# A hybrid decoder layer: the first projection piece by kinds of parts, key copies by DMA, and VectorE and GpSimd work given to ScalarE

## Chip, cores and metric

The kernel runs on one core of one Trainium2 chip. The metric is the device time of one execution in microseconds (us). Engine names are those of the profile: PE is TensorE, DVE is VectorE, ACT is ScalarE, POOL is GpSimd, SP is the engine that issues most DMAs; PEld is the loading of weights into TensorE.

## What is computed

One layer over 16 meta tokens and 1024 tokens of width 1024, in float32. Cut to what matters:

```python
u = rmsnorm(h, g_pre_mix)
q, k, v, xr, yr = split(u @ w_in)          # 512, 128, 128, 512, 512 columns
attn = sliding_window_attention_with_sinks(q, k, v, sinks)   # 8 heads of 64, 2 key heads, window 128
xr = causal_depthwise_conv(xr, conv_w, conv_b)               # 4 taps
hr = rg_lru(xr, w_a, b_a, w_x, b_x, lam)                     # gates, then a scan over the tokens
mix = concat([attn, gelu(yr) * hr]) @ w_out
h = h + rmsnorm(mix, g_post_mix)
f = square(relu(rmsnorm(h, g_pre_ffn) @ w_ff1)) @ w_ff2      # 4096 wide
h = h + rmsnorm(f, g_post_ffn)
return h without the meta tokens
```

## The kernel before

**Parts.** Every large operand is held as two float32r tiles: `hi`, the rounded value, and `lo`, what the rounding left. A product is three matmuls into one PSUM bank: hi·hi, hi·lo and lo·hi (`mm3`, L120 to L125; the projections are its lines 123, 124 and 125). As a rule ACT writes `hi` (a cast, L95, or a scaled copy, L116) and DVE writes `lo` (a subtraction, L98 or L117) after it.

**Order.** The engines run their own instructions in order. The order on each engine is fixed when the kernel is built, by a scheduler that looks at the whole program; `behind` and `lut` add pure order edges to it. Tiles come from pools of fixed depth by a letter ("a" 16, "b" 17, "c" 8, "d" 4, "e" 2, "raw" 2, "ws" 4), so a load can start only when the tile's earlier user is done.

**Stage 1, the first projections (0 to about 60 us).** The tokens are cut into four pieces of 256 columns (the first has 272, with the meta tokens). For each piece `normed` (L200 to L202) takes a row tile, squares and sums it on ACT, gets the reciprocal root on POOL (L158 adds EPS, L164 raises to the power -0.5), scales it on DVE; `transposed` (L242) turns it on PE, 8 blocks `kc` of 128 features, and ACT and DVE write the parts of `u` (L116, L117). Then four weights meet the piece: keys `wk`, values `wv`, the first query pair `wq`, the first recurrent chunk `wx`. `project` runs, for each `kc`, the three matmuls of that block. The sinks take the result out of PSUM: `put_k` writes each key head's `hi` into its own half of the partitions (ACT, L303), a second copy of it into the other half (DVE, L304), and its `lo` (DVE, L305). Attention needs both halves, since a query tile carries `hi` in one half and `lo` in the other.

**Stage 2, attention and the other projections (about 60 to 275 us).** For each of 4 head pairs and 2 halves, `scores` makes masked scores, exponentials (ACT, L82), and scales each of its 8 blocks of 128x256 by the reciprocal of the sum on DVE (L480). `attend` turns them and multiplies with the values. The other projections of queries, x and y are laid between as filling. `conv` runs per chunk on DVE: a first step that scales and adds the bias (L530), then three taps.

**Stage 3, recurrence gates, output projection, norms (to about 345 us), and stage 4, the two feed-forward products (to the end).** Both feed-forward products are done in seven block products instead of eight. In the second one, `fetch_2` (L1046 to L1060) loads each step's weight tile; where two tiles are summed, the second is loaded on top of the first by a POOL DMA that adds (L1055), or as a tile of its own. `LASTW` names the pools for the last eight steps.

**End.** The rows come out in two halves. Rows 512 to 1023 are finished during the last steps (`finish_early`). Rows 0 to 511, blocks j = 0 to 3, are finished after the last matmuls (`finish_half`, `finish_late`): add the last product (L788), sum of squares, reciprocal root, scale, add to the residual. For j = 0 and 1 the sum of squares is on ACT (L1117), the root on POOL (L160 on DVE, L164 on POOL), and a POOL DMA adds the block to the output (L1162). For j = 2 and 3 the residual is loaded ahead, the sum of squares is on DVE (L1165), the root on POOL (L1173), and the block is written by two plain DMAs (L1177, L1180). The last block's columns are done in two parts of 256.

Of the kernel before, what the change touches and what calls it, by code (L numbers as in the profile page):

```python
# [37 lines left out]
def hybrid_layer(  # L38
# [76 lines left out]
    def split_scaled(hi, lo, src, scale):  # L115
        nc.scalar.activation(hi, src, AF.Copy, scale=scale)  # L116
        nc.vector.scalar_tensor_tensor(  # L117
            lo, src, scale, f32(hi), op0=ALU.mult, op1=ALU.subtract
        )

    def mm3(dst, lhs, rhs, start, stop):
# [3 lines left out]
        nc.tensor.matmul(dst, ll, rh, start=False, stop=stop, skip_group_check=True)  # L125
# [29 lines left out]
    def rstd_of(ssq_parts, n=P):  # L155
# [8 lines left out]
        nc.gpsimd.tensor_tensor(rs[:n], ms[:n], half_pow[:n], op=ALU.pow)  # L164
# [32 lines left out]
    def norm_rows(src, n):  # L197
        xn = slot("d", [P, D])
        ssq = small.tile([P, 1], F32, name="ssq", tag="ssq")
        nc.scalar.activation(xn[:n], src, AF.Square, scale=RMS_SC, accum_out=ssq[:n])  # L200
        rs = rstd_of([ssq[:n]], n)
        nc.vector.tensor_scalar(xn[:n], src, rs, None, op0=ALU.mult)  # L202
        return xn
# [13 lines left out]

    ALL = [(0, 272), (272, 256), (528, 256), (784, 256)]
    REAL2 = [(16, 512), (528, 512)]

# [14 lines left out]
    def transposed(b, xn):  # L235
        t0, n = ALL[b]
        for kc in range(KC):
# [3 lines left out]
            for s, m in xn:  # L241
                nc.tensor.transpose(  # L242
                    pt[:, o : o + m], s[:m, kc * P : (kc + 1) * P], ident[:m, :m]
                )
                o += m
            uh, ul = u[kc]
            split_scaled(
                uh[:, t0 : t0 + n], ul[:, t0 : t0 + n], pt[:, :n],
                g_mix_col[:, kc : kc + 1],
            )  # L250

# [25 lines left out]
    wk = split_w(rk, "b")  # L277
    wv = split_w(rv, "b")
    transposed(0, xn)
    wq = split_w(rq)  # L280
    wx = split_w(rx)
# [7 lines left out]


    khh = [slot("b", [P, T], F32R) for _ in range(2)]
    kl = [slot("b", [P, T], F32R) for _ in range(2)]

    vk = [slot("b", [P, 8, P], F32R) for _ in range(2)]
    HALF = (slice(0, HD), slice(HD, P))
    vt = slot("c", [P, TT])
    for h in range(2):
        nc.gpsimd.memset(f32(kl[h][HALF[1 - h]]), 0.0)

    def put_k(hh, lo, src):  # L300
        for h in range(2):
            r, o = HALF[h], HALF[1 - h]
            nc.scalar.copy(hh[h][r], src[r])  # L303
            nc.vector.tensor_copy(hh[h][o], src[r])  # L304
            nc.vector.tensor_tensor(lo[h][r], src[r], f32(hh[h][r]), op=ALU.subtract)  # L305

    def sink_k(acc, t0, n):
        o = 0
        if t0 == 0:
            m = slice(0, NMETA)  # L310
            put_k(
                [km[:, 0, m], km[:, 1, m]], [km[:, 2, m], km[:, 3, m]], acc[:, m]
            )
            o = NMETA
        c = slice(t0 + o - NMETA, t0 - NMETA + n)
        put_k(
            [khh[0][:, c], khh[1][:, c]], [kl[0][:, c], kl[1][:, c]], acc[:, o:]
        )

    def sink_v(acc, t0, n):  # L320
        nc.scalar.copy(vt[:, t0 : t0 + n], acc)

    def new_q():
# [3 lines left out]
        def sink_q(acc, t0, n):  # L327
            c = slice(t0 - NMETA, t0 - NMETA + n)
            for h in range(2):
                r, o = HALF[h], HALF[1 - h]  # L330
                split_scaled(q[h][r, c], q[h][o, c], acc[r], HD ** -0.5)
# [10 lines left out]

    q0, sink_q0 = new_q()
    xr0, sink_x0 = new_x("c")
    for b in range(4):
        if b:
            transposed(b, normed(b))
        piece = [ALL[b]]
        project(wk, piece, sink_k)
        project(wv, piece, sink_v)  # L350
        project(wq, piece if b else [(16, 256)], sink_q0)
        project(wx, piece, sink_x0)
# [79 lines left out]
    def scores(j, half, q):  # L432
# [44 lines left out]
        for h in range(2):  # L477
            nc.vector.reciprocal(rden[:, h, :], den[:, h, :])
            for k in range(4):
                nc.vector.tensor_scalar(  # L480
                    sn[h][:, k, 0:256], sn[h][:, k, 0:256], rden[:, h, k : k + 1],
                    None, op0=ALU.mult,
                )
# [44 lines left out]
    def conv(c, xr, tag="d"):  # L528
        y = slot(tag, [P, TT])
        nc.vector.tensor_scalar(  # L530
            y, xr, prm[:, c, 3:4], prm[:, c, 4:5], op0=ALU.mult, op1=ALU.add
# [72 lines left out]
    nc.gpsimd.memset(graw, 0.0)  # L604
# [314 lines left out]

    for p in range(2):  # L920
# [361 lines left out]
```

## Time and profile before

| what | value |
|---|---|
| runs | 973.70, 974.02, 976.03 us; median 974.02 |
| profiled execution | 972.95 us; its span, first to last instruction, 971.1 us |
| PE busy | 953.7 us (98%), 4782 matmuls |
| DVE, ACT, POOL busy | 674.6, 502.0, 82.4 us |
| mean granted TensorE clock | 0.999 |
| HBM | 110.46 MB read, 18.87 MB written |

The profile page gives busy times by engine, the span in 40 slices, the DMA queues, the chain of work that ended last, and the costliest groups of instructions. Further views of the same trace: the list of who waited for whom, the timeline (start, duration, engine, line, operation, `out<-in`, shape, and in brackets the idle time before it and what ended it), and sums over windows of time. A matmul's duration in the timeline includes its way through the pipeline; the distance from one start to the next is what it costs.

### The profile page before, as it was taken

To read this page: it belongs to the slowest core of one execution; us is meant where nothing else is said; L and a number is where in the kernel's file an instruction comes from. 1 tells how busy PE (TensorE), PEld (TensorE's weight loads), DVE (VectorE), ACT (ScalarE), POOL (GpSimd) and SP (SyncE) were. 2 spreads that over 40 slices of the span, in tenths; PEclk is the share of its full clock that TensorE was granted. 3 is DMA by queue.
4 is the path that set the end of the run, shared out by engine and by line. 5 is a ranking of instruction groups with operands and counts; after the bars stand their busy time and mean duration, and the time that the engine had idled before them with its cause. 6 is when DMAs were issued, how large, how long until landed. Compare 5 with 4: busy or idle time off the path is not lost.

```text
span 971.1 us, 12490 instructions
## 1 busy us (share of the span) xinstructions
PE 953.7 (98%) x4782; PEld 803.0 (83%) x4782; DVE 674.6 (69%) x997; ACT 502.0 (52%) x809; POOL 82.4 (8%) x109
## 2 busy tenths in 40 slices
PE   6999999999999999999999999999999999999997
PEld 6999999888878887888888878888888888888786
DVE  6679997775976686665645465468557676779694
ACT  6646673567844554343555556555433344445350
POOL 4100000000002100000000000000111000003152
PEclk9999999999999999999999999999999999999999
DMA  9002001012234466576522264323678765548923
GB/s 296 23 1 66 23 23 44 23 48 64 84 119 144 159 207 209 173 251 209 198 87 87 97 206 125 114 87 114 172 176 198 186 224 187 184 163 195 223 80 87
DMA packets 88219, 130.13 MB, mean 134 GB/s; under 512 B 13624, under 2 KB 52552, under 8 KB 88160
## 3 DMA queue, kind: packets, MB, share of 16 engines
q1 hardware_dynamic: 79792, 107.33, 33.4%
q0 software_dynamic: 7792, 20.45, 10.1%
q10 hardware_dynamic: 576, 1.57, 0.4%
q8 instruction: 37, 0.61, 0.2%
q14 instruction: 22, 0.18, 0.1%
HBM read 110.46 MB, written 18.87 MB: 133 GB/s over the span
## 4 chain that ended last, share of the span: by engine, by line
PE 89%; DVE 4%; DMA 3%; issue 2%; ACT 1%; POOL 0%; SPq 0%; POOLq 0%; DVEq 0%; ACTq 0%
PE ps_acc L124 11%; PE ps_acc L123 11%; PE ps_acc L125 11%; PE ps_s L125 6%; PE ps_pt L123 6%; PE ps_s L124 6%; PE ps_pt L125 6%; PE ps_s L123 6%; PE ps_pt L124 6%; PE ps_o L124 5%; PE ps_o L123 5%; PE ps_o L125 5%; PE ps_o L506 2%; PE ps_pt L495 1%; DMA raw<-in_w_ff_dram 1%
## 5 line engine op out<-in xcount | busy, mean ns | idle before, releaser
L95 ACT CAST ws<-raw 128x1024 fp32r<-128x1024 f32 (+1 forms) x69 | 70.7, 1024 | 126.6 <-PE ps_o L124 48.8
L98 DVE TENSOR_TENSOR ws<-raw,ws 128x1024 fp32r<-128x1024 f32 (+1 forms) x70 | 83.5, 1194 | 59.6 <-ACT ws L95 59.5
L123 PE MATMUL ps_acc<-a,ws 128*128 128x256 f32 (+2 forms) x272 | 90.5, 333 | 0.6 <-DVE b L305 0.6
L124 PE MATMUL ps_acc<-a,ws 128*128 128x256 f32 (+2 forms) x272 | 89.8, 330 | 0.0
L125 PE MATMUL ps_acc<-a,ws 128*128 128x256 f32 (+2 forms) x272 | 89.4, 329 | 0.0
L98 DVE TENSOR_TENSOR b<-b,b 128x1024 fp32r<-128x1024 f32 (+2 forms) x48 | 57.6, 1201 | 24.7 <-PE ps_o L124 17.1
L95 ACT CAST ws<-e 128x1024 fp32r<-128x1024 f32 x43 | 45.0, 1046 | 55.3 <-PE ps_o L124 28.1
L95 ACT CAST b<-b 128x1024 fp32r<-128x1024 f32 (+2 forms) x48 | 49.4, 1030 | 42.8 <-DVE b L788 40.0
L98 DVE TENSOR_TENSOR ws<-e,ws 128x1024 fp32r<-128x1024 f32 x43 | 52.6, 1222 | 21.6 <-ACT ws L95 21.6
L123 PEld LDWEIGHTS ps_acc<-a,ws 128*128 128x128 f32 x272 | 51.2, 188 | 4.9 <-DVE b L305 0.8
L125 PEld LDWEIGHTS ps_acc<-a,ws 128*128 128x128 f32 x272 | 51.2, 188 | 4.6
L124 PEld LDWEIGHTS ps_acc<-a,ws 128*128 128x128 f32 x272 | 51.2, 188 | 3.9
L164 POOL TENSOR_TENSOR rs<-ms,half_pow 128x1 f32<-128x1 f32 (+1 forms) x31 | 21.3, 692 | 356.5 <-DVE ms L160 355.1
L123 PE MATMUL ps_acc<-ws,b 128*128 128x512 f32 (+1 forms) x120 | 46.3, 386 | 0.4 <-ACT ws L95 0.4
L124 PE MATMUL ps_acc<-ws,b 128*128 128x512 f32 (+1 forms) x120 | 46.5, 388 | 0.2 <-DVE ws L98 0.2
L125 PE MATMUL ps_acc<-ws,b 128*128 128x512 f32 (+1 forms) x120 | 46.2, 385 | 0.0
L123 PE MATMUL ps_pt<-ws,b 128*128 128x512 f32 x112 | 44.1, 394 | 0.0
L124 PE MATMUL ps_pt<-ws,b 128*128 128x512 f32 x112 | 44.1, 394 | 0.0
L125 PE MATMUL ps_pt<-ws,b 128*128 128x512 f32 x112 | 44.0, 393 | 0.0
L123 PE MATMUL ps_s<-ws,b 128*128 128x512 f32 x110 | 43.4, 395 | 0.0
L124 PE MATMUL ps_s<-ws,b 128*128 128x512 f32 x110 | 43.3, 393 | 0.0
L125 PE MATMUL ps_s<-ws,b 128*128 128x512 f32 x110 | 43.3, 393 | 0.0
(381 smaller groups left out, 2690.1 us busy)
## 6 DMA issues: line engine op xcount, KB each, us to landing
raw<-in_w_ff_dram SPq DMA_DIRECT2D x62, 512.0 KB, 4.0
e<-in_w_ff_dram SPq DMA_DIRECT2D x45, 512.0 KB, 3.6
d<-in_w_ff_dram SPq DMA_DIRECT2D x12, 512.0 KB, 3.8
s_dram<-d POOLq DMA_DIRECT2D x12, 512.0 KB, 3.9
raw<-in_w_in_dram SPq DMA_DIRECT2D x9, 512.0 KB, 3.6
c<-in_x_dram SPq DMA_DIRECT2D x8, 512.0 KB, 8.5
d<-in_x_dram SPq DMA_DIRECT2D x8, 512.0 KB, 4.6
out_dram<-raw SPq DMA_DIRECT2D x8, 512.0 KB, 2.6
```

The costliest lines, as they stand in the source:

```text
L95: nc.scalar.copy(hi, src)
L98: low = nc.vector.tensor_tensor(lo, src, f32(hi), op=ALU.subtract).ins
L123: nc.tensor.matmul(dst, lh, rh, start=start, stop=False, skip_group_check=True)
L124: nc.tensor.matmul(dst, lh, rl, start=False, stop=False, skip_group_check=True)
L125: nc.tensor.matmul(dst, ll, rh, start=False, stop=stop, skip_group_check=True)
L164: nc.gpsimd.tensor_tensor(rs[:n], ms[:n], half_pow[:n], op=ALU.pow)
L495: nc.tensor.transpose(pt[:, o : o + P], sn[h][:, 2 * bp + i, s * P : (s + 1) * P], ident,)
L506: nc.tensor.matmul(po[:, oc : oc + n], v, p_[:, pc : pc + n], start=first and k == 0, stop=last and k == 1, skip_group_check=True,)
```

## The change

1. First piece: the matmuls of a weight are ordered by kinds of parts (`part`): all eight hi·hi, then all eight with `lo` of `u`, then all eight with `lo` of the weight; keys and values share the first two kinds before either's third. The order of ACT and of DVE in this piece is written out (`chained`), the row tiles of the second piece are normed inside the first, and a later piece's transposes may not go ahead of the last matmul of the piece two before it.
2. Keys: the second copies leave DVE; after all four pieces four POOL DMAs copy the halves (two 64x1024, two 64x16). The zeroing of the keys' `lo` tiles moves to the start, that of `graw` behind the last power of the norms.
3. Half of the softmax scalings (odd blocks) and the first convolution step move from DVE to ACT.
4. Last norms: the root is a square root on ACT and a reciprocal on DVE, with no POOL; EPS is added on ACT; one instruction loads the table of the square root ahead of the first feed-forward product. Block j = 2 goes the way of j = 0 and 1 (squares on ACT, adding DMA).
5. `fetch_2`: from the third product on, the second tile of a step comes from pool "a"; the first of the last eight steps takes its tile from "b" and not from "raw".

```diff
+    def root_rstd(ssq, bias, n=P):
+        sd = small.tile([P, 1], F32, name="sd", tag="sd")
+        lut(sd[:n], ssq, AF.Sqrt, bias=bias)
+        rs = small.tile([P, 1], F32, name="rs", tag="rs")
+        nc.vector.reciprocal(rs[:n], sd[:n])
         return rs[:n]
...
+    def part(acc, w, piece, k, last=2):
+        t0, n = piece
+        for kc in range(KC):
+            last_mm[0] = nc.tensor.matmul(
+                acc[:, :n], w[k // 2][:, kc, :], u[kc][k % 2][:, t0 : t0 + n],
+                start=k == 0 and kc == 0, stop=k == last and kc == KC - 1,
+                skip_group_check=True,
+            ).ins.name
...
-    wk = split_w(rk, "b")
-    wv = split_w(rv, "b")
+    wk = high_w(rk, "b")
     transposed(0, xn)
-    wq = split_w(rq)
-    wx = split_w(rx)
+    low_w(wk, rk)
+    wv = high_w(rv, "b")
+    low_w(wv, rv)
+    wq = high_w(rq)
+    low_w(wq, rq)
...
-            nc.vector.tensor_copy(hh[h][o], src[r])
...
+            acc = [bank("acc"), bank("acc")]
+            for a, w in zip(acc, (wk, wv)):
+                part(a, w, piece, 0)
+                part(a, w, piece, 1)
+            xn = [(norm_rows(xt[2], P, True), P)]
+            part(acc[0], wk, piece, 2)
+            sink_k(acc[0][:, : piece[1]], *piece)
+            xn.append((norm_rows(xt[3], P, True), P))
+            part(acc[1], wv, piece, 2)
+            sink_v(acc[1][:, : piece[1]], *piece)
+            wx = high_w(rx)
+            low_w(wx, rx)
+            for w, (t0, n), sink in ((wq, (16, 256), sink_q0), (wx, piece, sink_x0)):
+                acc = bank("acc")
+                for k in range(3):
+                    part(acc, w, (t0, n), k)
+                sink(acc[:, :n], t0, n)
...
+    for h in range(2):
+        r, o, m = HALF[h], HALF[1 - h], slice(0, NMETA)
+        nc.gpsimd.dma_start(f32(khh[h][o]), f32(khh[h][r]))
+        nc.gpsimd.dma_start(f32(km[o, h, m]), f32(km[r, h, m]))
...
+                p_, r_ = sn[h][:, k, 0:256], rden[:, h, k : k + 1]
+                if k % 2:
+                    nc.scalar.activation(p_, p_, AF.Copy, scale=r_)
+                else:
+                    nc.vector.tensor_scalar(p_, p_, r_, None, op0=ALU.mult)
...
-        nc.vector.tensor_scalar(
-            y, xr, prm[:, c, 3:4], prm[:, c, 4:5], op0=ALU.mult, op1=ALU.add
+        nc.scalar.activation(
+            y, xr, AF.Identity, scale=prm[:, c, 3:4], bias=prm[:, c, 4:5]
         )
...
-    nc.gpsimd.memset(graw, 0.0)
+    behind(last_pow[0], nc.gpsimd.memset(graw, 0.0).ins)
...
+    load_root()
...
-        ("raw", None), ("e", "raw"), ("b", None), ("b", None), ("raw", "e"), ("b", None),
+        ("b", None), ("e", "raw"), ("b", None), ("b", None), ("raw", "e"), ("b", None),
...
-        tags = (("raw", "e"), ("e", "raw"))[n % 2] if i < 6 else LASTW[q]
+        tags = LASTW[q]
+        if i < 6:
+            tags = ("raw", "e")[n % 2], "a" if i > 1 else ("e", "raw")[n % 2]
...
-            if j < 2:
+            if j < 3:
                 w_low[0] = nc.vector.scalar_tensor_tensor(
-                    o, acc, rstd_of([squares(o[:, c], acc[:, c], 0), ssq]), gffn_b,
+                    o, acc, root_rstd(squares(o[:, c], acc[:, c], 0), ssq), gffn_b,
                     op0=ALU.mult, op1=ALU.mult,
...
-        rs = small.tile([P, 1], F32, name="rs", tag="rs")
-        nc.gpsimd.tensor_tensor(rs, ssq, half_pow, op=ALU.pow)
-        c = COLS[0]
-        combine(o[:, c], acc[:, c], gffn_b[:, c], ALU.mult)
+            if k == 1:
+                rs = root_rstd(ssq, 0.0)
+            w_low[0] = combine(o[:, c], acc[:, c], gffn_b[:, c], ALU.mult).name
```

## The prediction

> **What bounds the kernel now.** I read the page's busy times and slices first, then the list of PE's waits, then the timelines of the first 30 us and of the end.
>
> ```profile
> PE 953.7 (98%) x4782; PEld 803.0 (83%) x4782; DVE 674.6 (69%) x997; ACT 502.0 (52%) x809; POOL 82.4 (8%) x109
> ...
> PE   6999999999999999999999999999999999999997
> ```
>
> PE is full in 38 of 40 slices: work moved between other engines in the middle can only cost. Time can be won only in the first slice, in the last, and in PE's few waits:
>
> ```profile
> PE ps_s L242 <- DVE d L202: 5.8, 1, 5.8
> PE ps_o L242 <- DVE d L202: 1.4, 2, 0.7
> ...
> PE ps_acc L123 <- ACT a L971: 0.7, 1, 0.7
> PE ps_acc L123 <- DVE b L305: 0.6, 1, 0.6
> PE ps_pt L123 <- ACT b L95: 0.4, 1, 0.4
> PE ps_acc L123 <- ACT ws L95: 0.4, 1, 0.4
> PE ps_acc L124 <- DVE ws L98: 0.2, 1, 0.2
> ```
>
> Apart from the start that is 2.3 us; L971 at 364 us and `b L95` at 271 us are not touched by the change. Now the start:
>
> ```profile
> 8.40 1.52 DVE L202 TENSOR_SCALAR d<-c,rs 128x1024 f32<-128x1024 f32 x1 [0.77 <-POOL rs L164]
> 8.43 2.38 POOL L298 MEMSET b<- 64x1024 f32 x2
> 9.85 2.34 DVE L98 TENSOR_TENSOR b<-raw,b 128x1024 fp32r<-128x1024 f32 x2
> 10.49 0.49 ACT L116 ACTIVATE a<-ps_o,gcol 128x272 fp32r<-128x272 f32 x1
> ...
> 13.81 0.43 PE L123 MATMUL ps_acc<-a,b 128*128 128x272 f32 x1
> 14.04 0.43 PE L124 MATMUL ps_acc<-a,b 128*128 128x272 f32 x1
> ...
> 20.13 0.29 PE L125 MATMUL ps_acc<-a,b 128*128 128x272 f32 x1
> 20.25 0.28 PE L123 MATMUL ps_acc<-a,b 128*128 128x272 f32 x1
> ```
>
> Two things are to be seen. DVE computes both weights' `lo` (2.34 us) before any `lo` of `u`, so PE's order hi·hi, hi·lo, lo·hi cannot run until 13.1. And a 128x272 matmul costs 0.226 us at 13.8 and 0.125 us at 20.1: PE runs at about half rate until 19.2 us, though the page's granted clock is 9 throughout. So an early start of PE counts about half until the rate doubles.
>
> **The change, part by part.** Instruction orders are those that the built kernels have.
>
> *First piece (1), and the zeroing (2).* The two memsets (2.38 us) now precede the norms on POOL. The first token tile's root comes about 0.35 us later, the second's not later (its squares end at 7.3), and its scaling takes 0.75 instead of 1.52 us (other L202 rows: 0.75), done at 9.16. PE's transposes of it are then held by those of the first tile, to about 9.4; the first `hi` of `u` starts at 9.9 (transpose to ACT: 0.51, as 9.98 to 10.49), 0.6 earlier. Eight at 0.38 end at 13.05; PE's hi·hi for the keys end at 13.35. DVE's eight `lo` at 0.41, now ahead of the weights' `lo`, end near 13.8; the keys' weight `lo` at 15.0, the values' at 16.2. So from 13.35 PE has no wait: 32 matmuls up to the end of the keys. When does the rate double? Before, the unbroken run began at 14.85 (after a wait of 0.25), 4.35 us before 19.2; counted from 13.14, 6.05 us. I take 4.35: 17.7. Up to there 4.35/0.226 = 19 matmuls; the other 13 at 0.125 give 1.6: keys done at t = 19.3.
>
> From there ACT sets the pace. It has, in order: two key copies (0.37 each) and two small ones (0.17), two squares (1.24 each with their read), the values' copy (0.5), then the cast of `wx` (1.05): t + 5.25. PE meanwhile has 8 matmuls, 6 transposes (0.109 each) and 24 for `wq` (0.119): t + 4.5, so it waits 0.75, taking the place of the 0.8 that PE lost at 27.2 to 28.1. Then 24 matmuls of 0.125 and 6 transposes: the second piece's keys start at t + 9.0 = 28.3. Before, they started at 31.97, with 16 more transposes done (1.74): equal work at 30.23. **Gain 2.0.** With 6.05: t = 20.05, gain 1.2. If the scattered matmuls from 10.4 on already count: doubled at 14.75, t = 18.0, gain 3.3.
>
> The Trainium skill (TensorE: Matmul & The Clock Gate, Part 1) says that the array runs at half rate until it has been busy for one window of about 3.4 us, and that the window runs freely. The trace's 0.226 and 0.125 agree. By that rule the run from 13.35 doubles between 16.75 and 20.15, a gain of 2.4 to 0.9, and it would vary from run to run.
>
> *Key copies (2).* DVE loses 8 x 0.42 + 2 x 0.17 = 3.7 us where PE waits no more: 0. The copies are new waits of the scores. Nearest row: a POOL DMA of 512 KB, 3.0 to 5.7 us from issue to landing. After the last keys: ACT 0.4, POOL's two issues of about 0.5 each, landing at 4.4 to 7.1. PE has 65 matmuls and 9 small ones first, 8.6 us. Price 0; bound 1 us if a copy shared the queues with a weight load. The 64x16 copies hold POOL's queue, ahead of two norms' roots, at about t + 1.2 to t + 3; those are needed at t + 7: 0. `graw` now holds three weight loads on SP until about 41 us; the first is used at about 76: 0.
>
> *Scalings and convolution (3).* DVE loses 32 x 0.35 + 4 x 0.82 = 14.5 us. ACT gains 32 blocks (nearest rows: 0.48 from PSUM, 0.51 for the exponential) and 4 x about 1.1: 20 us over 60 to 200 us, where it is busy 83 of 140 (DVE 119, PE 140). No PE wait is there to be removed: gain 0. Cost between 0 and 8 us (below); I take 0, since ACT comes to 74%.
>
> *Tile for the first of the last steps (5).* The wait at 917 us:
>
> ```profile
> 907.68 9.19 DMA raw<-in_w_ff_dram
> 916.96 1.05 ACT ws L95
> 918.03 1.24 DVE ws L98
> ```
>
> This chain of waits shows the adding DMA landing at 916.9, because its base waited for a "raw" tile until 903. Matmul starts lose 0.58 (917.25 to 918.05) and 0.34 (918.86 to 919.31). In the new order the base is issued ahead of the one that went at 889.7, and its addition stands before two others on POOL: **gain 0.9**. Next late is a plain load in the slot that comes free at 903, needed after 919.
>
> *Last norms (4).* One table load, 1.28 us, where ACT is half busy: 0. For j = 3, POOL's 1.1 us (965.18 to 966.29) go; instead a square root (nearest 128x1 row: 0.19) and a reciprocal (0.17). But j = 2 now puts a 1.28 us scaling on DVE where two of 0.7 stood, behind a sum of squares on ACT. Counting DVE's queue from the last key row: add 961.92, scaling 962.34 to 963.62, squares of part 0 to 964.2, product 964.6, add 965.0 (PE is done at 964.0), squares to 965.6, product 966.0, scaling of j = 3 at 966.15 instead of 966.31: **gain 0.15**. The adding DMA of j = 2 is issued 0.7 after 963.62 and lands 5.1 later (the row at 959.98): 969.4, against 970.2 for j = 3.
>
> **Sum:** 2.0 + 0.9 + 0.15 = 3.05. Span 971.1 to 968.05, profiled time 972.95 to 969.9. The median of the runs is 1.07 above the profiled execution, so 974.02 - 3.05 = **971.0 us**.
>
> **Rivals.**
> - *The doubled rate comes late, or ACT's chain is longer:* the start gives 1.2 and the 917 us stall comes back by half at the next load. 974.0 - 1.8 = 972.2. For it: the 6.05 us that before needed from 13.14. Against: before's run was broken at 14.7.
> - *The doubled rate comes early:* 3.3 at the start, 974.0 - 4.35 = 969.7. For it: PE is already two-thirds busy from 9.4 on; against: before it was so too from 10 to 13, and it did not help.
> - *Slower: ACT is late in attention.* Every head pair and half puts four odd scalings on ACT, where a weight cast (1.05) or the next exponentials (0.69 each) may stand ahead of them, and the transposes of that block wait. Eight halves, each late by one cast: 8 x 1.05 = 8.4, 979.4. It decides from 3.05/8 = 0.4 us a half on. For it: ACT is at 14.6 and 14.8 of 20 us in the windows 80 to 100 and 120 to 140. Against: transposes follow the scalings by filling matmuls.
> - *The end is set by the new adding DMA:* if the two plain DMAs of j = 3 slow it by 2 us, it lands at 971.4, 1.2 later: 972.2 with the rest. Before, j = 1's met j = 2's plain ones and landed in 5.1, against j = 0's 5.0 without them.
> - *The change does not do what it says:* the key copies land late by as much as the start wins, 974.0. Needs 10.6 us instead of 4.4 to 7.1.
>
> **Chances.** Forecast 0.42, late rate 0.20, early rate 0.18, ACT late 0.08, adding DMA 0.07, key copies 0.05. 0.3% is 2.9 us, about what a measurement of this kernel can tell from no change, and the forecast lies on that edge: I give it 0.24 above and 0.18 below. Faster by over 0.3%: 0.24 + 0.18 = 0.42. Slower: the ACT case and a little, 0.09. Same: 0.49. Range: from the early rate with a lucky phase and 0.7 us of scatter, 968.5, up to the key-copy case, 974.0; the ACT case is left out.
>
> **What would show it.** First `hi` of `u` at 9.9; distance of matmul starts falling to 0.125 at about 17.7; PE's only later wait of the start on ACT's cast of `wx`, 0.75 us; no wait of scores on a DMA; no wait at 917; last scaling of j = 3 at 0.15 earlier after PE's end. PE waits between 60 and 270 us, or a start that wins under 1 us, would make it wrong.

## The result: slower, and the profile after

The changed kernel takes 983.34 us (median; 982.01 to 985.21), the kernel before 974.26 on the same chip: ratio 1.0088, 95% interval 1.0073 to 1.0104. Forecast was 971.0. The profiled execution took 983.86 us, its span is 982.1.

The page's busy times and PE's slices, after:

```profile
PE 955.1 (97%) x4782; PEld 801.6 (82%) x4782; DVE 659.1 (67%) x949; ACT 524.0 (53%) x865; POOL 65.1 (7%) x105
...
PE   6999999999899999999999999999999999999996
```

PE has the same 4782 matmuls and nearly the same busy time (before: 953.7), so the time was lost between matmuls. The list of PE's waits, after (us in total, times, longest):

```profile
PE ps_o L153 <- DMA e<-in_g_pre_ffn_dram: 6.7, 1, 6.7
PE ps_acc L125 <- DVE ws L98: 5.2, 4, 1.7
PE ps_pt L124 <- ACT b L95: 2.7, 1, 2.7
PE ps_o L618 <- DVE c L98: 0.8, 1, 0.8
...
PE ps_o L618 <- ACT c L95: 0.7, 1, 0.7
...
PE ps_o L124 <- ACT c L82: 0.6, 1, 0.6
```

The first line is the start; the others are new or larger. Where they lie: `ws L98` once at 718 us and three times from 826 to 840; `b L95` at 265; the two of L618 at 148 and 150; `c L82` at 225.

**265 us.** ACT's timeline, after:

```profile
265.45 1.28 ACT L82 ACT_TABLE_LOAD   x1
266.74 0.20 ACT L82 ACTIVATE root<-eps_col 128x1 f32<-128x1 f32 x1
266.85 1.03 ACT L95 CAST a<-d 128x1024 fp32r<-128x1024 f32 x1
267.79 0.61 ACT L95 CAST b<-d 128x512 fp32r<-128x512 f32 x1
```

The scheduler has put `load_root` right behind the last Gelu. Behind it stands a weight's cast, and behind that the cast that PE needs. PE's timeline, and its granted clock in windows (time, PE busy and matmuls, clock, DMA share, GB/s):

```profile
268.45 0.80 PE L124 MATMUL ps_pt<-a,b 128*128 128x512 f32 x1 [2.71 <-ACT b L95]
269.05 0.63 PE L125 MATMUL ps_pt<-a,b 128*128 128x512 f32 x1
269.47 0.63 PE L124 MATMUL ps_pt<-a,b 128*128 128x512 f32 x1
```

```profile
268.00:270.00 2.00, 1.55 (x4) 0.61 0.00 0
270.00:272.00 2.00, 2.00 (x7) 0.54 0.78 264
```

The stop itself loses 2.86 us of starts (the one before is at 265.36, and a 128x512 matmul costs 0.23). Behind it such a matmul costs 0.42 us (269.05 to 269.47) instead of 0.23, for about eight of them: 1.6 us more. The rows show idle time of 2.7 us followed by some 3.4 us at half clock. The Trainium skill (TensorE: Matmul & The Clock Gate, Part 1) states that an idle window of about 3.4 us takes the clock back to half, and that the window runs freely. The half rate agrees; here less than one window of idleness was enough (the last section works out how much).

**826 to 840 us.** One of three like stops: a sum on DVE and the low part behind it, SP's next loads, and PE's wait for that low part:

```profile
832.01 1.23 DVE L900 TENSOR_TENSOR raw<-raw,a 128x1024 f32<-128x1024 f32 x1 [4.01 <-issue]
833.15 1.22 DVE L98 TENSOR_TENSOR ws<-e,ws 128x1024 fp32r<-128x1024 f32 x1
```

```profile
833.26 0.37 SPq L1173 DMA_DIRECT2D a<-in_w_ff_dram  x1
834.40 0.37 SPq L1173 DMA_DIRECT2D e<-in_w_ff_dram  x1
```

```profile
834.43 0.50 PE L125 MATMUL ps_acc<-ws,b 128*128 128x512 f32 x1 [1.67 <-DVE ws L98]
```

Each load into "a" is issued at the end of the sum that frees that tile (832.01 + 1.23 = 833.24, then 833.26). The load into "e" or "raw" is issued at the end of the low part that stands behind the sum (833.15 + 1.22 = 834.37, then 834.40; the list of SP's waits names this low part), and the next sum waits for loads that were just issued (4.01 us idle here, 3.35 and 3.66 at the neighbours). So load, sum, low part and next load form a chain: the three sums start at 824.51, 832.01 and 838.86, about 7 us apart. In the kernel before, the low part stands ahead of the sum (818.62 and 819.76), and its sums at 803.45 to 831.57 are 5.6 us apart on average.

**The start** won more than was forecast: the second piece's keys start at 27.42 (forecast 28.3, equal work before 30.23), a gain of 2.8. In t1_plain_j2 below, whose start is the same code, they start at 29.34, a gain of 0.9. The last 45 matmuls of the first piece's keys and values, here and there:

```profile
13.06 6.20 PE L252 MATMUL ps_acc<-a,b 128*128 128x272 f32 x45
```

```profile
13.47 7.74 PE L252 MATMUL ps_acc<-a,b 128*128 128x272 f32 x45
```

The difference is the rate. Here it doubled at 12.4 us, in t1_plain_j2 at 17.6: starts there are 0.227 apart until 17.5 and 0.125 after it, and the traces' records of the clock begin at these two times (the page counts the time before the first record as full clock). The 917 us stall is gone.

To follow the gain I use landmarks that every kernel passes once: V, ACT's copy of the third piece's values; G, the first 128x348 matmul (recurrence gates); F, the first 128x512 matmul `<-b,e` after 280 us (early in the first feed-forward product); E, the span's end. Before: V 51.08, G 204.20, F 350.80, E 971.1. Differences to that, one profiled execution each, and the median over that of the kernel before on the same chip:

```
                      V      G      F      E    median
after               -3.5   +0.1   +4.4  +11.0   +9.1
e1_no_a             -4.0   +1.1   +5.4   +6.0   +5.4
e2_root_late        -3.4   +0.1   +1.4   +6.3   +7.5
e3_dve              -2.0   +1.2   +2.7   +9.1   +7.3
t1_plain_j2         -1.6   +2.0   +6.2  +10.6   +8.6
q3_old_sink_q_alone -2.9   +0.5   +1.2   +6.1   +5.8
q5_mended           -2.7   +2.1   +1.9   +3.0   -0.6
q6_mended_dve       -3.0   +1.5   +1.3   +1.0   +0.7
p1_first_piece      -0.9   +2.9   +3.5   +5.6   +4.7
p2_keys_dma         -3.8   +2.0   +2.6   +5.2   +4.3
q2_old_sink_q       -3.1   +2.9   +2.7   +4.0   +2.9
o1_swap             -1.4   +1.2   +2.0   +3.5   +3.7
b1_end_only         +0.5   +0.6   +0.6   +0.6   -0.5
```

V is a matter of order too. By V the kernel before and b1_end_only have done 62 transposes of 128x128, the other twelve 54, at 0.109 us each: 0.9 us of every gain at V is work put off. In o1_swap, with the start's work unchanged, that is 0.9 of the 1.4; the other 0.5 is there by the end of the first piece, and its rate doubled at 17.3 us, before's at 19.3. So after: 3.5 ahead at V (2.6 at equal work), level at 204, 4.3 more lost by 351, and 6.6 from there to the end.

### The profile page after: what moved, and what is told of

Same layout as the page of the kernel before. It is cut to its first block, busy times and chain, and to the rows that moved or that the text cites. A ratio compares the mean times of both kernels' runs of the same rounds, so it can differ in the third digit from the quotient of the medians.

```text
span 982.1 us, 12496 instructions
## 1 busy us (share of the span) xinstructions
PE 955.1 (97%) x4782; PEld 801.6 (82%) x4782; DVE 659.1 (67%) x949; ACT 524.0 (53%) x865; POOL 65.1 (7%) x105
## 5 line engine op out<-in xcount | busy, mean ns | idle before, releaser
L95 ACT CAST ws<-raw 128x1024 fp32r<-128x1024 f32 (+1 forms) x68 | 69.6, 1023 | 120.7 <-PE ps_o L125 62.0
L98 DVE TENSOR_TENSOR ws<-raw,ws 128x1024 fp32r<-128x1024 f32 (+1 forms) x69 | 82.2, 1192 | 41.1 <-ACT ws L95 40.9
L124 PE MATMUL ps_acc<-a,ws 128*128 128x256 f32 (+2 forms) x256 | 85.7, 335 | 0.2
L126 PE MATMUL ps_acc<-a,ws 128*128 128x256 f32 (+2 forms) x256 | 85.7, 335 | 0.0
L125 PE MATMUL ps_acc<-a,ws 128*128 128x256 f32 (+2 forms) x256 | 85.3, 333 | 0.0
L95 ACT CAST ws<-e 128x1024 fp32r<-128x1024 f32 x41 | 42.9, 1045 | 64.3 <-PE ps_o L125 51.4
L98 DVE TENSOR_TENSOR b<-b,b 128x1024 fp32r<-128x1024 f32 (+2 forms) x48 | 57.5, 1199 | 21.0 <-PE ps_o L125 13.5
L95 ACT CAST b<-b 128x1024 fp32r<-128x1024 f32 (+2 forms) x48 | 49.4, 1029 | 38.6 <-DVE b L900 38.6
L98 DVE TENSOR_TENSOR ws<-e,ws 128x1024 fp32r<-128x1024 f32 x41 | 50.1, 1222 | 15.4 <-ACT ws L95 15.4
L124 PEld LDWEIGHTS ps_acc<-a,ws 128*128 128x128 f32 x256 | 48.3, 189 | 4.5 <-ACT c L396 0.4
L126 PEld LDWEIGHTS ps_acc<-a,ws 128*128 128x128 f32 x256 | 48.2, 188 | 4.3
L125 PEld LDWEIGHTS ps_acc<-a,ws 128*128 128x128 f32 x256 | 48.2, 188 | 3.9
L124 PE MATMUL ps_acc<-ws,b 128*128 128x512 f32 (+1 forms) x120 | 46.2, 386 | 0.0
L124 PE MATMUL ps_pt<-ws,b 128*128 128x512 f32 x112 | 44.3, 395 | 0.0
L124 PE MATMUL ps_s<-ws,b 128*128 128x512 f32 x110 | 43.5, 395 | 0.0
L124 PE MATMUL ps_o<-ws,b 128*128 128x512 f32 (+1 forms) x108 | 41.4, 383 | 0.0
```

The source lines that it names most:

```text
L95: nc.scalar.copy(hi, src)
L98: low = nc.vector.tensor_tensor(lo, src, f32(hi), op=ALU.subtract).ins
L124: nc.tensor.matmul(dst, lh, rh, start=start, stop=False, skip_group_check=True)
L125: nc.tensor.matmul(dst, lh, rl, start=False, stop=False, skip_group_check=True)
L126: last_mm[0] = nc.tensor.matmul(dst, ll, rh, start=False, stop=stop, skip_group_check=True).ins.name
```

## The experiments

Theory at first: each added part brings a wait of its own, and the costs add. Rival: the earlier start changes what meets what, and the parts only show it. The first four undo one part each, or make one alone. A median's difference to the kernel before is uncertain by about 1.5 us (half a 95% interval of 0.15%), a difference between two such by about 2, so the medians alone do not tell the 1.6 (e2_root_late), 1.8 (e3_dve) and 0.5 (t1_plain_j2) below from nothing; there the place in the profile is the evidence.

### e1_no_a

```diff
-            tags = ("raw", "e")[n % 2], "a" if i > 1 else ("e", "raw")[n % 2]
+            tags = (("raw", "e"), ("e", "raw"))[n % 2]
```

> The changed kernel, with fetch_2's second tile taken from the pools raw and e again, so that no weight load waits for a sum that frees a tile of pool a (the first load of the last feed-forward pass keeps its tile of pool b). Theory (each added part costs its own wait): TensorE's waits of 1.87 us near 718 and of 0.95, 1.84 and 1.18 us near 826, 832 and 840 on VectorE's low parts are gone, and nothing takes their place: 983.3 - 5.8 = 977.5 us. Rival (the earlier start shifts what meets what, and the tiles only show it): the waits stay or move, and the time stays within 1.5 us of 983.3.

979.29 us, 5.4 over the kernel before instead of 9.1: 3.7 us less. All four waits on `ws L98` are gone. On DVE the low part again stands ahead of the sum, so the load goes out when the sum ends (821.49 + 1.23 = 822.72, then 822.74), and the sums are 5.7 us apart on average (815.62 to 838.36):

```profile
819.85 1.22 DVE L98 TENSOR_TENSOR ws<-raw,ws 128x1024 fp32r<-128x1024 f32 x1 [1.87 <-ACT ws L95]
821.49 1.23 DVE L900 TENSOR_TENSOR raw<-raw,e 128x1024 f32<-128x1024 f32 x1 [0.41 <-DMA raw<-in_w_ff_dram]
```

```profile
822.74 4.26 SPq L1173 DMA_DIRECT2D e<-in_w_ff_dram  x2
```

The theory holds. The size, 3.7 instead of 5.8, differs by about what two medians can; in the profiles E falls by 5.0, though this execution ran at half rate once more, behind the waits near 148 us (below).

### e2_root_late

```diff
-        lut(root, eps_col, AF.Sqrt)
+        behind(mark[0], lut(root, eps_col, AF.Sqrt))
...
-    load_root()
     for p in range(2):
         p1(p, a11_early[p])
...
+    load_root()
     LAST = 3
```

> The changed kernel, with load_root (the square root's table and its one-element use) placed behind a low part just ahead of the last feed-forward loop, instead of where ScalarE's last Gelu leaves it. Theory: the wait of 2.7 us near 265 on ScalarE's cast, with the matmuls at half rate behind it (8 of 0.42 instead of 0.23 us, 1.6 us), was made by the table load (1.28), the root (0.20) and the cast that stood behind them: it falls to 0.6 us as before the change, and the time to 983.3 - 3.5 = 979.8 us; the load costs nothing in its new place. Rival: the wait is the two casts' own (1.0 and 0.6 us), which the shift brought there; it stays above 1.5 us and the time is above 982 us.

981.39 us, 7.5 over: 1.6 less. In the profile F falls from +4.4 to +1.4, 3.0 us: the wait at 265 is 1.2 and the clock stays at 1.00. The theory holds for the place, with 1.2 instead of 0.6 left; the median is 1.6 above its 979.8.

### e3_dve

```diff
-                if k % 2:
-                    nc.scalar.activation(p_, p_, AF.Copy, scale=r_)
-                else:
-                    nc.vector.tensor_scalar(p_, p_, r_, None, op0=ALU.mult)
+                nc.vector.tensor_scalar(p_, p_, r_, None, op0=ALU.mult)
...
-        nc.scalar.activation(
-            y, xr, AF.Identity, scale=prm[:, c, 3:4], bias=prm[:, c, 4:5]
+        nc.vector.tensor_scalar(
+            y, xr, prm[:, c, 3:4], prm[:, c, 4:5], op0=ALU.mult, op1=ALU.add
```

> The changed kernel, with all softmax scalings and the first convolution step on VectorE again. Theory: the two starts lost near 148 and 149.5 us (0.96 and 0.90) go, those of 225 us (0.8, a sigmoid behind casts) may go too: 983.3 - 2.0 to -3.0 = 980.3 to 981.3 us. Rival (VectorE was relieved, and gets the work back: 16 scalings of 0.28 and 8 steps of about 0.7 us): waits on VectorE take their place, and the time is 983 us or above.

981.25 us, 7.3 over: 1.8 less. But the loss near 150 us did not go. It became 0.6 (`ps_o L615 <- ACT c L95`) and 2.1 (`ps_acc L124 <- ACT d L422`), while the wait at 265 fell to 0.6. Neither theory fits: the median is the theory's, the place is not.

### p1_first_piece

The change's start on the kernel before, without items 3 to 5, and the keys' second copies on DVE:

```diff
     def low_k(hh, lo, src):
...
+        for h in range(2):
+            r, o = HALF[h], HALF[1 - h]
+            inss.append(nc.vector.tensor_copy(hh[h][o], src[r]).ins)
...
-        nc.gpsimd.dma_start(f32(khh[h][o]), f32(khh[h][r]))
```

> The kernel before, with the first piece by kinds of parts alone (the keys' second copies on VectorE as before, the memsets moved, nothing of the other parts). Theory: the second piece's keys start at about 27.5 instead of 30.2 us (equal work), the 2.8 us stay gained to the end, where the wait at 917 us stays as it was: 974.3 - 2.8 = 971.5 us. Rival (the shift by itself makes the later waits, or gives the gain back at waits on ScalarE and DMA): 974 us or above, with new waits after 140 us.

978.67 us, ratio 1.0048 (1.0035 to 1.0061): slower by 4.7 us with nothing added but the part that was to win. This is the rival's result, and it changed the question. Two of PE's waits, and the clock behind the second:

```profile
PE ps_acc L124 <- ACT d L426: 2.0, 1, 2.0
PE ps_acc L252 <- ACT c L400: 1.8, 1, 1.8
```

```profile
22.00:24.00 2.00, 1.80 (x11) 0.72 0.63 144
24.00:26.00 2.00, 2.00 (x11) 0.50 0.93 227
```

The wait on L400 is at 20 us and is followed by half rate, so the start wins 0.9 and not 3. The wait on L426 is at 153 us, where no instruction was changed. The built kernels show why: the scheduler has set the projections and the attention in another order, from the second piece on.

What makes it do so? `sink_q`, which the change rewrites for the first piece (the list of its items does not name this), serves every later query pair too: both casts now stand ahead of both subtractions. New theory: the order of the attention is what costs.

### o1_swap

```diff
             for h in range(2):
-                r, o = HALF[h], HALF[1 - h]
-                split_scaled(q[h][r, c], q[h][o, c], acc[r], HD ** -0.5)
+                r = HALF[h]
+                nc.scalar.activation(q[h][r, c], acc[r], AF.Copy, scale=HD ** -0.5)
+            for h in range(2):
+                r, o = HALF[h], HALF[1 - h]
+                nc.vector.scalar_tensor_tensor(
+                    q[h][o, c], acc[r], HD ** -0.5, f32(q[h][r, c]),
+                    op0=ALU.mult, op1=ALU.subtract,
+                )
```

> The kernel before, with one thing of the change: sink_q writes both halves' casts ahead of both subtractions instead of by turns. The scheduler then sets the projections and the attention in nearly the order of TensorE that the run with the first piece alone had (it differs from the kernel before from the second piece on). Theory (the order costs, not the work): the waits of that run come back near 153 us (2.0 us, with half rate behind it) and near 745 us, and the time is 973.9 + 3.5 to 5 = 977.4 to 979 us, with no gain at the start. Rival (the swap moves nothing that counts, and the first piece alone lost by its own work, VectorE's copies of the keys ahead of the wait of 1.8 us at 20 us and the half rate behind it): 974 us, within 1 us.

978.12 us, ratio 1.0035 (1.0021 to 1.0049). The same instructions, two of them exchanged in a sink, cost 3.7 us. PE's waits show p1's at 153 us again (and one of 0.8 on `ws` at 760):

```profile
PE ps_acc L123 <- ACT d L345: 2.0, 1, 2.0
```

Of some 1600 matmuls from 30 to 275 us, compared by tile and shape, 99% stand in p1_first_piece's order and 51% in before's. PE waits there for ACT to copy x out of PSUM; ACT waits for the "d" tile that the convolution's last tap on DVE still reads.

### o2_pinned

PE's instructions, from the second piece to the end of the attention, are tied one to the next in the order of the kernel before (order edges, no semaphores). The first piece is by kinds, keys on DVE, `sink_q` old.

```diff
+    for runs in ORDER:
+        names = [f"I-{a + d * k}" for a, n, d in runs for k in range(n)]
+        for before, name in zip(names, names[1:]):
+            behind(before, nc.made[name])
```

> The first piece by kinds on the kernel before (keys' second copies on VectorE, sink_q as before), with TensorE's instructions from the second piece to the end of the attention held in the order of the kernel before by ordering links that carry no semaphore. Theory (the order costs): the waits near 153 and 745 us are gone, and what the first piece gains at the start stays, 0.6 us as in the run without links or up to 2.8 us where the wait of 1.8 us at 20 us goes too: 971.1 to 973.3 us. Rival (the first piece's own work costs): 977 us or above, as without links.

977.78 us, 3.3 over: the rival's time, but not the rival's place. All 16 copies of the attention's results on ACT, from 83 to 218 us, are later than before's by 2.5 to 2.7 us: the attention lost nothing. The 2.6 were lost ahead of it, by the wait of 1.8 at 20 us and its half rate, and by 0.55, 1.07 and 0.54 us at 31 to 33, where the old order asks for the third piece's transposes before they are ready. So the old order costs nothing in the attention, and it does not fit the new start.

### o3_pinned_b

The same, and `LASTW[0]` is "b" (item 5's second half).

> The kernel of the pinned run, and the first load of the last feed-forward pass from pool b as in the change. Theory: the wait of 0.58 us near 917 us on ScalarE's cast and the one of 0.34 behind it go, 0.9 us less than the pinned run: 970.2 to 972.4 us. Rival: what follows is late in its place, and the time is that of the pinned run.

982.33 us, 7.9 over and 4.6 more than o2_pinned; both expectations miss. POOL and DVE near 910 us (rows of PE, DVE and ACT carry the line of a helper that records instructions, L47):

```profile
909.34 1.05 POOL L239 TENSOR_TENSOR rs<-ms,half_pow 128x1 f32<-128x1 f32 x1
```

```profile
910.42 1.28 DVE L47 SCALAR_TENSOR_TENSOR a<-b,rs,a 128x1024 f32<-128x1024 f32 x1 [9.03 <-POOL rs L239]
```

A last norm's root stands on POOL behind an adding DMA that is issued only at 908.58; DVE stands behind the root for 9 us, and PE loses 4.7 us to the `ws` part behind that and runs at half rate from 911.4 to 918.2 us. With the roots on ACT (items 4 and 5 together) the same tile is harmless, as b1_end_only shows.

### o4_act_pinned

The kernel before with item 3 (edit as in e3_dve, reversed) and PE's order held as in o2_pinned.

> The kernel before, with the odd softmax scalings and the first convolution step on ScalarE as in the change, and TensorE's instructions of the projections and the attention held in the order of the kernel before. Theory (the order costs, and ScalarE has room for the work): no new wait over 0.3 us between 60 and 260 us, and 973.9 us, within 1 us. Rival (the scalings and steps are late on ScalarE): starts lost on ScalarE's casts at each block, as 0.95 and 0.90 us near 148 us in the changed kernel, and 976 us or above.

974.80 us, ratio 1.0005 (0.9992 to 1.0017). With before's order the scalings and steps on ACT cost nothing that can be told. They do show: the wait on the cast `b L95` is 1.3 us (near 265 us) instead of 0.4 (near 271 us).

### p2_keys_dma

p1_first_piece with the keys' copies by DMA, as in the change.

> The kernel before, with the first piece by kinds and the keys' second copies by DMA, and nothing else of the change. Theory (the copies on VectorE are what held back the start of the run with the first piece alone: TensorE's wait of 1.8 us near 20 us on ScalarE's copy of the values, and 1.7 us of half rate behind it): that wait is 0.3 to 0.9 us, the granted clock stays at 1.00 from 22 to 28 us, the start gains some 3 us more than with the copies on VectorE, and the order of the attention (with its 0.9 and 2.3 us near 150 us as in the run with the scalings on VectorE) takes them back: 973 to 976 us, against 978.7 with the copies on VectorE. Rival (it does not count who copies the keys): 978 us or above.

978.31 us, 4.3 over: the copies' way does not count at the end. It counts at the start: V is -3.8 instead of -0.9, the wait at 20 us is 0.5 and the clock stays at 1.00. The attention took this back: 0.6 and 2.1 us of waits at 149 and 152, as in e3_dve, and here half rate behind them. p2_keys_dma, then e3_dve:

```profile
152.00:156.00 4.00, 3.17 (x15) 0.50 0.01 4
```

```profile
152.00:156.00 4.00, 1.92 (x16) 1.00 0.01 4
```

Nearly the same order, the same two waits, and only one of the two executions pays for them twice. The last section shows why.

### q2_old_sink_q

p2_keys_dma with `sink_q` as before.

> As the run with the first piece and the keys by DMA, with sink_q as before the change (cast and subtraction by turns), which gives another order of the projections and the attention. Theory (the order that the rewritten sink_q leads to is what costs near 150 us): no wait over 0.5 us between 100 and 200 us, and 970 to 972 us. Rival (each new order meets late casts somewhere, and the order of the kernel before was a good one among many): other waits of 2 to 4 us between 60 and 260 us, and the time within 1.5 us of that run.

976.89 us, 2.9 over: the rival. Its waits near 122 us (0.7 and 0.2) and 152 to 156 us (0.9, 0.4) are others, the loss from V to G is no smaller (-3.1 to +2.9), with half rate from 156 to 159.6 us in it. Whatever makes the order, it lost what the start had won.

### t1_plain_j2

The changed kernel with j = 2 by two plain DMAs:

```diff
-        if j > 2:
+        if j > 1:
             h = slot("d", [P, D])
...
-            if j < 3:
+            if j < 2:
```

> The changed kernel, with the next to last row block (j = 2) written by two plain DMAs from a sum with the loaded rows again, its square root as in the change. Theory (its adding DMA of 512 KB shares the queues with the last block's two plain DMAs, which land 3.5 instead of 2.6 us after their issue): the last DMAs land 2.6 us after issue, and 983.3 - 0.7 = 982.6 us. Rival (the end of the changed kernel is longer for another reason, one more instruction on VectorE ahead of the last block): 983.3 us, within 0.5, or above.

982.67 us, 8.6 over instead of 9.1. The last scaling in the chain of waits, after and then in t1_plain_j2:

```profile
976.21 0.75 DVE a L1293
```

```profile
976.82 0.75 DVE a L1293
```

From the last scaling to the span's end it is 5.9 us after (982.1 - 976.21) and 4.9 here (981.7 - 976.82); before it was 4.8. That is the theory's place and size, 0.5 to 1.0; the median alone would not settle it. In after the plain write on ACT's queue takes 3.5 us from issue to landing, before and here 2.6.

### q5_mended

The changed kernel with e1's, e2's and t1's edits, and `sink_q` as before.

> The changed kernel, with four things mended together: no tile of pool a for the loads, the root's table load just ahead of the last feed-forward loop, block j = 2 by plain DMAs, and sink_q as before; scalings and the first convolution step stay on ScalarE, the keys' copies on DMA, and the last norms by square roots. Theory (the costs add): 983.3 - 4.0 - 2.0 - 0.7 = 976.6 us if the order of the attention costs what it costs in the changed kernel, and down to 973 us if the new order has no waits near 147 us. Rival (they overlap: what one mend wins shows at the next wait): 978 us or above.

973.43 us, ratio 0.9991 (0.9978 to 1.0004): 9.7 us less than the change, and level with the kernel before. Undone one by one the four gave 3.7, 1.6, 0.5 and 3.3 (below), 9.1 in all. Two of the waits left, near 150 us:

```profile
PE ps_acc L125 <- ACT d L417: 1.0, 1, 1.0
PE ps_o L613 <- DVE c L99: 0.9, 1, 0.9
```

### q3_old_sink_q_alone

> The changed kernel with sink_q as before (cast and subtraction by turns), and nothing else undone. Theory (the mends of the mended run add: 4.0 for the tiles of pool a, 2.0 for the table load, 0.7 for block j = 2 leave 3.2 us of its 9.9 for the order): 983.3 - 3.2 = 980.1 us, within 1 us. Rival (the order is worth nothing by itself, the mends overlap): 982.5 us or above.

979.56 us, 5.8 over: 3.3 less than the change, by two exchanged instructions. Where the order shows: ACT's timeline has the same table load at the same place in its queue, but 4 us earlier, and PE then waits only 0.7 and 0.6 us:

```profile
261.40 1.28 ACT L82 ACT_TABLE_LOAD   x1
...
263.74 0.62 ACT L95 CAST b<-d 128x512 fp32r<-128x512 f32 x1
```

So the loss at 265 us had two conditions, the load and an order that brought ACT there late; taking away either wins 3.0 to 3.2 at F.

### o5_pinned_dma, o6_pinned_act, q6_mended_dve, o7_all_pinned

The first is o2_pinned with the keys copied by DMA after each piece; the second adds item 3; the third is q5_mended with item 3 undone (in the scheduler's order); the fourth is q5_mended with the copies after each piece and before's PE order.

> The first piece by kinds on the kernel before, with the keys' second copies by DMA, now piece by piece, sink_q as before, and TensorE's instructions from the second piece to the end of the attention held in the order of the kernel before. Theory (the order decides whether the start's gain is kept): no wait of 1.8 us at 20 us, up to 2 us of waits near 32 us where the order of before asks for the third piece's transposes early, none over 0.5 us from 80 to 260 us, and what is gained at 80 us stays to 290 us: 971 to 973.5 us. Rival (ScalarE and VectorE bound the attention, so that TensorE waits for them as long as it came earlier): waits between 80 and 260 us that give the gain back, and 974 us or above.

> As the pinned run with the keys by DMA, with the odd scalings and the first convolution step on ScalarE. Theory (with an order that suits them they cost nothing, as in the pinned run on the old start): within 1 us of the run without them. Rival (ScalarE is late for an earlier start): 2 us more than it, with waits on ScalarE's casts near 150 us.

> The mended kernel (no tile of pool a, table load late, block j = 2 plain, sink_q as before), with the softmax scalings and the first convolution step on VectorE again, in the scheduler's own order. Theory (the work's engine counts for nothing by itself, the order that comes out of it does): between 972 and 976.5 us, with other waits near 120 to 158 us than the mended run's (0.9 and 1.0 us near 150). Rival (moving the work to ScalarE is a gain by itself): 975 us or above, with waits on VectorE.

> The mended kernel with scalings and step on ScalarE, keys' copies by DMA piece by piece, and TensorE's order of the projections and the attention held as in the kernel before. Theory (the order decides, the mends add): 2 us less than the mended run's 973.4, that is 970.5 to 972.5 us. Rival (the mended run's waits near 150 us are ScalarE's and VectorE's own): 973.4 us or above.

977.80, 979.17, 974.85 and 977.64 us: 3.6, 5.0, 0.7 and 3.5 over. The pinned three miss their theories at one place: the 16 landmarks of the attention lie 1.2, 3.3 to 3.8 and 2.0 to 2.4 us behind before's, apart from three in each of the two with item 3 that are up to 3.0 more; and they lie there already at 83 us (o6_pinned_act and o7_all_pinned ran at half rate from 33 to 36.5 us, o5_pinned_dma did not). So neither theory nor rival has the place: the loss is ahead of the attention. In the new start PE does all of the first piece before the second piece's transposes; the old order had them mixed, and held to it PE no longer wins: V is then 52.42 in o5_pinned_dma, 1.3 behind before. The gain and the old order exclude each other in these forms. (Of the 3.6 of o5_pinned_dma the rest is the stall near 920 us, 2.1 here and with half rate behind it.) Item 3 adds 1.4 in o6_pinned_act, between the two expectations. q6_mended_dve is as expected; against q5_mended it says that ScalarE or VectorE makes no difference that can be told (0.7 and -0.6).

### b1_end_only

The kernel before with `LASTW[0]` "b", the roots by square root and reciprocal with the late table load, j = 2 plain.

> The kernel before, with the end of the change alone, mended: the first load of the last feed-forward pass from pool b, the last norms by square root and reciprocal with the table load just ahead of the last feed-forward loop, block j = 2 by plain DMAs. The orders of all engines up to there are those of the kernel before. Theory: the 0.9 us of the wait near 917 us and 0.2 to 0.4 us at the end are won: 974.2 - 1.2 = 973.0 us, within 0.6 us. Rival (the loads that move with the tile are late, as in the pinned run with pool b): 974.5 us or above.

973.26 us, 0.5 less, ratio 0.9993 (0.9981 to 1.0005): not to be told from no change, though on the expected side. No wait is left at 917. A wait of 1.2 us on a low part near 775 us stands here and not in before's profile; no run says why.

## Why the prediction was wrong

By its own steps:

- **Start (2.0):** a gain of the right kind, its size set by luck. After won 2.8 at equal work since its rate doubled at 12.4 us, earlier than the early rival's 14.75. In t1_plain_j2 it doubled at 17.6, close to the forecast's 17.7, and the gain was 0.9: the steps before were too hopeful. The first `hi` of `u` came at 10.4 (before 10.5) and not at 9.9, and in t1_plain_j2 PE had done three of the keys' hi·hi by 13.47, not eight by 13.35. PE's later wait was not on ACT's cast of `wx` (0.75) but on DVE's part of the keys (`km`), 0.55 and 0.91. Over ten executions with the keys by DMA and the scheduler's order the rate doubled between 11.2 and 17.6 us, and V is 4.0 to 1.6 earlier, the less the later the rate doubled (q5_mended alone stands out of line, by 0.3). The Trainium skill (TensorE: Matmul & The Clock Gate, Part 1) says that the window runs freely, so that the doubling moves from run to run, by 500 ns either way; the trace agrees on the first and shows 6.4 us for the second.
- **"Sum: span 971.1 to 968.05" is the step that failed first.** It carries the start's gain to the end because PE is full from there on. But PE being full does not fix the order of its work, and the change gave the scheduler another program. p1_first_piece shows the part that was to win 2.0 losing 4.7; o1_swap shows 3.7 of loss from an edit with no work in it; q3_old_sink_q_alone takes 3.3 back from the change by the same edit. The prediction read the new order for single steps, and never compared the attention's order as a whole.
- **Scalings and convolution (0):** the price was right (o4_act_pinned 0.3, q5 against q6), the ground, half-empty ACT, only in part: the wait on `b L95` is 0.9 longer in o4_act_pinned. The waits near 148 us are the order's: with the work back on DVE they only change place. The rival of eight late halves did not happen.
- **Last norms, "where ACT is half busy: 0":** failed. The load costs 1.28 us on an engine whose next cast PE waits for. With the order it cost 1.6 (median, e2_root_late) to 3.0 (at F), half of that by the clock. The Trainium skill (ScalarE: Activation LUTs, What ACT_TABLE_LOAD costs) gives 1.28 us for the load and 1.38 us for a drain; here the next instruction starts 1.29 after the load's start (265.45 to 266.74), so the 1.28 agrees and no drain shows.
- **The tiles of item 5:** not priced at all. The prediction costed "b" and passed over "a". It was the largest single loss, 3.7 us. The step that was missing: who frees the tile, which load waits for that, and what stands on DVE between that load's sum and the next load.
- **Tile for the first of the last steps (0.9):** right where the roots are on ACT (no wait at 917 after, in e1, q5 and b1). o3_pinned_b shows that it is not a property of the tile.
- **End (0.15 gain):** wrong sign. The last scaling did come earlier behind PE's last start, by 0.5 (2.12 us instead of 2.59), but the writes behind it took 1.1 longer. The rival that the adding DMA of j = 2 meets j = 3's plain ones came about, at 0.5 to 1.0 us instead of 1.2; the plain ones are the ones that show it.
- **Key copies (0):** right at the end of the kernel; what DVE's copies cost is a stop of 1.8 us and the half rate behind it at 20 us.
- **Small slips:** of the 2.3 us of waits "apart from the start" 0.6 (`b L305`, near 28 us) lie in the start, and ACT's terms add up to t + 5.1 and not 5.25. Nothing in the result rests on them.

So 9.1 is, by medians: tiles 3.7, order and table load together about 5.5 (one by one 3.3 and 1.6), the adding DMA 0.5, less 0.6 for all the rest. Each part is uncertain by about 2 us, and the 5.5 is what q5_mended's 9.7 leaves for it. **Open:** whether an order exists that keeps the start's 3 us. Each order that the scheduler made with the new start lost 3 to 6 us from V to G (0.9 of it the transposes put off, and 1.6 or 3.2 of it half rate in e1_no_a, q5_mended, p1_first_piece, p2_keys_dma and q2_old_sink_q); before's own order does not go with that start. No run had both.

## What to carry to other kernels

Where a scheduler orders the engines, an edit's price has two parts, its work and the order that comes out; compare the built orders far from the edit, and test the second part by an edit that has no work in it. Price every queue that a moved load stands in, and what its consumer's engine does before it frees the next tile: here load, sum, low part and next load became one chain of about 7 us a step, where 5.6 was the pace before. A table load is not filling: put it where nothing that a full engine waits for stands behind it.

## What the runs showed of the hardware

- **Where the clock can change.** In all 20 profiles every change of the granted clock lies a whole number of steps of 3.413 us behind the first rise of its execution. Where the first step lies differs from execution to execution: among ten starts with the same work the first rise is at 11.2 to 17.6 us.
- **What makes it fall.** It is PE's idle time summed within one such step, and not the longest stop. Idle is here what the distance between two starts has beyond the usual one of that shape (0.231 us for 128x512, 0.118 for 128x256). While PE had work, the clock fell to half behind 17 steps, with 2.03 to 3.33 us idle in each. It stayed full behind the other 5546 steps at full clock, with at most 1.94 us idle in all but one (2.05, e3_dve). So one stop of 1.8 us at 20 us (p1_first_piece) was enough with small ones beside it.
- **Why it looks like chance.** After and e1_no_a have the same two waits near 148 and 150 us, 0.84 and 0.73. In after the border of two steps, 148.96, parts them (1.11 and 1.53 us idle); in e1_no_a one step has most of both (2.13), and the clock falls behind it. Likewise one step of p2_keys_dma has 2.34 us, none of e3_dve more than its 2.05. After, then e1_no_a (start and end of the step, its length, PE busy and matmuls, clock, DMA share, GB/s):

```profile
145.54:148.96 3.42, 2.58 (x23) 1.00 0.00 0
148.96:152.37 3.41, 2.57 (x18) 1.00 0.00 0
```

```profile
147.75:151.16 3.41, 2.02 (x12) 1.00 0.00 0
151.16:154.57 3.41, 3.41 (x18) 0.50 0.02 5
```

- **What it costs.** The half rate lasts one step, 3.41 us, or two (p2_keys_dma, o3_pinned_b), and a step of it costs a full PE about 1.6 us (the eight matmuls behind 268 us), as much as such a wait itself. o3_pinned_b has four such steps, some 6 us, so one profiled execution can stand that far from the next; how far a median of a few runs moves is not shown.
